# Trainium2, a two-layer decoder trunk in split fp32: the first weights and the first block of x in halves, another order of forms, warm-up products from a constant

## The chip, the cores and the metric

The kernel runs on one core of one Trainium2 chip, in one launch. The metric is the time of that launch on the device, in microseconds (us). An execution recorded by the profiler gives the trace and the profile from which rows are quoted. The engines in them are PE (TensorE, matrix products), PEld (its weight loads), DVE (VectorE), ACT (ScalarE), POOL (GpSimd) and SP (SyncE, which here only issues DMAs). A "q" behind an engine's name (SPq, POOLq) means the DMA queue that it feeds.

## What is computed

A residual stream x of 256 rows and 4096 columns goes through two layers, each with its RMS norm, and a final RMS norm:

```
def reference(x, norm_attn, w_in_attn, w_out_attn, norm_conv, w_in_conv, conv_w,
              w_out_conv, final_norm):
    h = x
    for i in range(DEPTH):
        if i % N_MIXERS == 0:
            h = h + attn_branch(rms_norm(h, norm_attn), w_in_attn, w_out_attn)
        else:
            h = h + conv_branch(rms_norm(h, norm_conv), w_in_conv, conv_w, w_out_conv)
    return rms_norm(h, final_norm)

def attn_branch(xn, w_in, w_out):
    proj = xn @ w_in
    q, k, v, g = jnp.split(proj, 4, axis=-1)
...
    o = stick_breaking_attention(to_heads(q), to_heads(k), to_heads(v))
...
    return (o * jax.nn.silu(g)) @ w_out
```

`DEPTH` is 1, so only the attention branch is computed: an input projection (256 x 4096 by 4096 x 16384), a causal attention of 32 heads of 128, a gate, an output projection (4096 x 4096), the residual sum, and the final norm with its gain. All inputs are float32.

## The kernel before

**Tiling.** The output of a projection is made in units (`units`, line 279): 16 units of `w_in`, each of two pairs of column blocks of 256, and then the units of `w_out`. A unit runs over 16 steps of the contraction (`NS`), each of 2 x 128 (`KT` = 2). For a step there are two tiles of weights, `raw{q}_{t}`, each 128 partitions x 2 column blocks x 2 contraction halves x 256 float32, 512 KB, fetched on SP's queue by two DMAs of one column block each (`load`, line 380). Seven such tiles can be in memory at once. All of x stays in memory as 16 blocks of 128 x 2 x 256 (`blocks_of`, line 553), one for each step.

**Split operands.** Every operand is used as a high part and a low part in a type of reduced precision: for weights, ACT casts `raw` into `wh` and DVE subtracts, giving `wl` (`piece`, line 451). x's forms in the first unit are `sh` and `sl`, in the other units `nh` and `nl`; those of the attention's output are `oh` and `ol`. A product is three matmuls of 512 columns into a bank `acc`: high by high, high by low, low by high (`mm3`, line 816). The numbers behind these names count the parts (`wl930` is the low part of part 930). Most steps are done with sums of blocks in seven products in place of eight (`SEVEN_PARTS`, line 84); for those DVE also forms sums of `raw` tiles (`sums`, line 424), and POOL adds one block onto another by a DMA that accumulates (`add_block`, line 401).

**What sets the order.** The products follow each other on PE in one list (`order`, line 306). Everything else is ordered by a planner (`Plan`, line 113), which simulates the engines with estimated costs while the program is written: a piece of work asks for buffers (`take`), waits until something is told (`until`, `tell`), and queues for its engine with a key, mostly the estimated time of the product that needs it. When an engine of the simulation comes free, the work with the lowest key is written into the real program (`turn`, line 229). On the chip each engine then executes its instructions in this order, and semaphores keep the true dependences. A different estimate or one more wait at the start thus can alter what the planner does anywhere behind it.

**The start.** x's block 0 takes the gain and one DMA of 256 KB on ACT's queue (lines 576 and 577). For each contraction half DVE forms `sh`, then waits for the low part of the weights of that half, then forms `sl` (lines 581 to 592). The first weight part (n = 0) is cut into halves (line 489) and its low part waits for `sh` (line 469), so that DVE makes `sh`, `wl`, `sl` twice. After that the raw block 0 is scaled with the gain by ACT (lines 597 to 601) for its sums. Blocks 1 to 3 of x are requested at fixed planned times (line 565). Ahead of the first product PE multiplies tiles of zeros, `idle`, into a bank `warm` that nobody reads; DVE sets each of the ten (lines 614 to 618).

**The end.** In the last unit the last five parts are kept, and their products run bank by bank in the order 5, 4, 2, 3 (`LAST_ORDER`, line 60). h stands in 16 tiles `h0` to `h7` for each of two halves of the rows, t = 0 and t = 1. `last_h` (line 1107) and `block_done` (line 1142) add the banks to h and the rows of x (`xres`); bank 3 is added to `h7` of t = 0 in two halves of 256 columns, behind the last products. For each t the sums of squares give a factor: `mean_before_last` (a reduce and a tensor_scalar), `joined` (a scalar_tensor_tensor), and in `finish` (line 1184) the `factor` of four operations, all on the tile `scalars`. `rows_out` (line 1206) then multiplies each tile of h by it, and SP stores the tile, 256 KB each. The rows of t = 1 are done first.

Almost all instructions bear one line number in the profile, L132, which is the helper that records them; the names of the tiles tell them apart.

Of the kernel before, what the change touches and what calls it, by code (L numbers as in the profile page):

```python
# [12 lines left out]
BF16 = mybir.dt.bfloat16  # L13
# [6 lines left out]
P = 128  # L20
S = 256
# [4 lines left out]
CW = 256  # L26
HG = CW // P
NB = D // CW
W = 2 * CW
NJ = D // W  # L30
KT = 2
# [6 lines left out]
BEHIND = {("turn", 0): ("eee", "eee")}  # L38
WARM, IDLE = 10, 640

# [12 lines left out]
ROWS = 4  # L53
# [195 lines left out]
def kernel(  # L249
# [10 lines left out]
    nc = Plan(tc)  # L260
# [50 lines left out]
    for g, (n, k) in enumerate(order):  # L311
        p = parts[n]
# [60 lines left out]
    raw, wh, wl = {}, {}, {}  # L373
# [6 lines left out]
    def load():  # L380
# [3 lines left out]
        for _, q, t in sorted(tiles):  # L384
            w, blocks, s = quads[q][t]
            if FORMS_BEHIND < q < NS:
                yield nc.until(("form", "s", q - FORMS_BEHIND))
            yield nc.take("raw")
            r = raw[q, t] = wp.tile([P, HG, KT, CW], F32, tag="raw", name=f"raw{q}_{t}", bufs=RAW_BUFS)
            if t and seven[q]:  # L390
                nc.start(add_block(q))

            def both():
                for i, c in enumerate(blocks):
                    nc.sync.dma_start(r[:, i], w[c, s])

            yield moved(
                "sync", both, [KT * CW] * HG, first[quad_parts[q][0]] + t, after=lambda q=q, t=t: nc.tell(("raw", q, t))
            )
# [51 lines left out]
    def piece(n, c, there):  # L451
# [16 lines left out]
        if n == 0:  # L468
            yield nc.until(("sh", c.start))
        yield dve(lambda: minus(l, full, h), size, key, more=10)  # L470
# [4 lines left out]
    def split(size, tag, bufs):  # L475
        for n, p in enumerate(parts):
# [4 lines left out]
            if size == KT:  # L481
                yield nc.take(tag)
            yield nc.until(("raw", q, t))
            if size < KT:
                yield nc.take(tag)
            wh[n] = halves(wp.tile([P, KT * W], F32R, tag="wh" if size == KT else "s", name=f"wh{n}", bufs=bufs))
            if size == 1:
                wh[n], wl[n] = wh[n][:, 0:1], wh[n][:, 1:2]
            cuts = [slice(k, k + 1) for k in range(KT)] if n == 0 else [slice(0, size)]
            lows_left[n] = len(cuts)  # L490
            if p["seven"] and p["i"] == 0:
                nc.start(sums(q))
            for c in cuts:
                nc.start(piece(n, c, [("sums", n)] if p["seven"] and p["i"] > 1 else [("raw", q, t)]))

# [57 lines left out]
    def blocks_of(i):  # L553
# [9 lines left out]
        if i:  # L563
            yield moved(
                "sync", lambda: nc.sync.dma_start(y, xT[i]), [KT * S], key - 1, hold=True, wait=1300 * i - 600 if i < 4 else 0
            )
# [8 lines left out]
        else:  # L575
            yield moved("scalar", lambda: nc.scalar.dma_start(gcol, gain_in), [KC], key - 1)
            yield moved("scalar", lambda: nc.scalar.dma_start(y, xT[i]), [KT * S], key - 1, hold=True)
            for c in range(KT):
                hc, lc = (t[:, 2 * c : 2 * c + 2, :].rearrange("p a b -> p (a b)") for t in (h, l))

                yield dve(
                    lambda: nc.vector.tensor_scalar(out=hc, in0=y[:, c, :], scalar1=gain(c), scalar2=None, op0=ALU.mult),
                    S, key - 1,
                )
                nc.tell(("sh", c))
                yield nc.until(("low", 0, c))
                yield dve(
# [3 lines left out]
                    S, key - 1,  # L591
                )
        nc.tell(("form", "s", i))
        later = place_at(0, i + BLOCKS_LATER)
        if not i:

            def scaled():
# [16 lines left out]
    warm = att.tile([P, W], F32, tag="att", name="warm")  # L614
    for k in range(WARM):
        idle = wp.tile([P, IDLE], BF16, tag="gh", name=f"idle{k}", bufs=ROWS)
        nc.vector.memset(idle, 0.0)
        nc.tensor.matmul(warm, idle[:, 0:P], idle[:, 0:W], start=True, stop=True)

# [195 lines left out]

    def mm3(out_, a, b, start, stop, orders):

        (ah, al), (bh, bl) = a, b
        for k, (x, y) in enumerate(((ah, bh), (ah, bl), (al, bh))):
            q, e = RUNS[orders[k]]  # L820
# [418 lines left out]
    def product(n, k):  # L1239
# [7 lines left out]
        elif p["i"] == 0 and k == 0:  # L1247
# [7 lines left out]
            ends[p["u"], b] == (n, k),  # L1255
            orders,
        )

# [80 lines left out]
```

## Time and profile before

| | before |
|---|---|
| median of three runs | 1693.62 us |
| the three runs | 1691.8, 1693.62, 1694.25 us |
| profiled execution: span from its first to its last instruction | 1691.3 us |
| median less that span | 2.3 us |
| DMA moved in the span | 412.78 MB, mean 244 GB/s |

The profiled execution is known by its span; the time around it is taken as the difference in the table's fourth row. In the rows that follow, a timeline's columns are the start in us, the length from the first instruction's start to the last one's end, engine, line, operation, output<-inputs with their shapes, and the number of instructions joined in the row (x10); in brackets stand the idle time ahead of it and what ended it. Rows of the waits give the total, the count and the longest. A row of windows gives the stretch and its length, then the busy time and the count of PE, PEld, DVE, ACT and POOL in this order, then the granted clock, the busy share of the DMA engines and their GB/s. Rows of transfers give the issuing queue, size, and us from issue to landing.

### The profile page before, as it was taken

Reading aid. Unit: us, or ns where it says so; the run is one execution under the profiler, and the core shown is the slowest. Engines: PE = TensorE matmul, PEld = TensorE weight load, DVE = VectorE, ACT = ScalarE, POOL = GpSimd, SP = SyncE. Lnnn points to the kernel's source line nnn. Section 1 sums busy time; section 2 is a strip of 40 time slices with the busy share of each in tenths; the row PEclk is TensorE's granted clock in tenths of the full one; section 3 lists DMA queues with packets and bytes.
Section 4 is the critical chain, followed back from the end, with each engine's and each line's share of the span. In section 5 each row is a group of like instructions: output and inputs, shape, how many; then the busy total and the mean of one; then the engine's idle time right before and its main releaser. Section 6 shows DMA issues by size and latency. Waiting matters only on the chain.

```text
span 1691.3 us, 25185 instructions
## 1 busy us (share of the span) xinstructions
PE 1675.4 (99%) x7776; PEld 1419.6 (84%) x7776; DVE 1599.4 (95%) x2025; ACT 1200.8 (71%) x1665; POOL 325.5 (19%) x400
## 2 busy tenths in 40 slices
PE   9999999999999999999999999999999999999996
PEld 7888888888888888888888888888888888888885
DVE  8889999999999999999999999999999987999997
ACT  8986767676767686867676767686867775666664
POOL 0012222222212222222222222212122111212110
PEclk9999999999999999999999999999999999999999
DMA  9978887889788979797979787878787877888895
GB/s 344 331 199 244 235 240 222 242 234 251 223 242 229 260 210 256 216 268 201 267 207 268 210 259 214 258 216 250 220 252 223 282 259 245 245 246 262 246 302 186
DMA packets 248440, 412.78 MB, mean 244 GB/s; under 512 B 28016, under 2 KB 72560, under 8 KB 248304
## 3 DMA queue, kind: packets, MB, share of 16 engines
q1 hardware_dynamic: 194544, 354.24, 62.6%
q0 software_dynamic: 53472, 56.65, 20.3%
q8 instruction: 61, 1.00, 0.2%
q14 instruction: 75, 0.61, 0.1%
q10 hardware_dynamic: 288, 0.28, 0.1%
HBM read 402.93 MB, written 8.13 MB: 243 GB/s over the span
## 4 chain that ended last, share of the span: by engine, by line
PE 97%; DVE 1%; DMA 1%; issue 0%; ACT 0%; SPq 0%; DVEq 0%; ACTq 0%
PE acc L132 92%; PE z L132 3%; PE o L132 1%; PE tr L132 1%; DMA raw<-in_w_in_dram 1%; DVE h L132 0%; DVE wl L132 0%; ACT wh L132 0%; DVE raw L132 0%; DVE scalars L132 0%; SPq L132 0%; DVE qk_sb L132 0%; ACT sq L132 0%; ACT scalars L132 0%; DVE sl L132 0%
## 5 line engine op out<-in xcount | busy, mean ns | idle before, releaser
L132 ACT CAST wh<-raw 128x1024 fp32r<-128x1024 f32 (+1 forms) x989 | 916.0, 969 | 375.9 <-DVE raw L132 166.2
L132 DVE TENSOR_TENSOR wl<-raw,wh 128x1024 fp32r<-128x1024 f32 (+1 forms) x815 | 967.4, 1216 | 44.6 <-ACT wh L132 25.3
L132 PE MATMUL acc<-wh,sh 128*128 128x512 f32 x2048 | 768.8, 387 | 0.3 <-DVE sh L132 0.3
L132 PE MATMUL acc<-wh,sl 128*128 128x512 f32 x1898 | 727.2, 383 | 0.1
L132 PE MATMUL acc<-wl,sh 128*128 128x512 f32 x1748 | 668.6, 382 | 0.0
L132 POOL DMA_DIRECT2D raw<-in_w_in_dram x300 | 259.0, 962 | 972.9 <-DMA raw<-in_w_in_dram 472.4
L132 PEld LDWEIGHTS acc<-wh,sh 128*128 128x128 f32 x2048 | 384.2, 188 | 69.1 <-ACT wh L132 1.2
L132 PEld LDWEIGHTS acc<-wh,sl 128*128 128x128 f32 x1898 | 356.0, 188 | 64.4 <-DVE sl L132 0.9
L132 PEld LDWEIGHTS acc<-wl,sh 128*128 128x128 f32 x1748 | 328.5, 188 | 56.8 <-DVE wl L132 0.4
L132 DVE TENSOR_TENSOR raw<-raw,raw 128x512 f32<-128x512 f32 x348 | 237.7, 683 | 7.6 <-DMA raw<-in_w_in_dram 5.9
L132 PE MATMUL acc<-wh,oh 128*128 128x512 f32 x512 | 192.2, 383 | 0.0
L132 PE MATMUL acc<-wh,ol 128*128 128x512 f32 x488 | 186.6, 382 | 0.0
L132 PE MATMUL acc<-wl,oh 128*128 128x512 f32 x464 | 177.4, 382 | 0.7 <-DVE wl L132 0.7
L132 DVE TENSOR_TENSOR wh<-raw,wh 128x512 fp32r<-128x512 f32 x174 | 118.7, 682 | 0.6 <-ACT wh L132 0.3
L132 DVE TENSOR_TENSOR raw<-raw 128x512 f32<-128x512 f32 x174 | 118.7, 682 | 0.0
L132 PEld LDWEIGHTS acc<-wh,oh 128*128 128x128 f32 x512 | 96.0, 187 | 17.2
L132 PEld LDWEIGHTS acc<-wh,ol 128*128 128x128 f32 x488 | 91.5, 187 | 16.1
L132 PEld LDWEIGHTS acc<-wl,oh 128*128 128x128 f32 x464 | 87.0, 188 | 16.9 <-DVE wl L132 1.4
L132 POOL DMA_DIRECT2D raw<-in_w_out_dram x48 | 41.7, 985 | 173.7 <-DMA raw<-in_w_out_dram 69.8
L132 ACT ACTIVATE f<-f 128x384 f32<-128x384 f32 x96 | 50.4, 525 | 3.0
L132 DVE SCALAR_TENSOR_TENSOR gv_sb<-acc,scalars,gv_sb 128x512 f32<-128x512 f32 x45 | 33.5, 744 | 0.3
L132 POOL DMA_DIRECT2D p<-spill x27 | 16.1, 662 | 87.8 <-ACT wh L132 27.1
(86 smaller groups left out, 765.3 us busy)
## 6 DMA issues: line engine op xcount, KB each, us to landing
raw<-in_w_in_dram SPq DMA_DIRECT2D x1024, 256.0 KB, 4.5
raw<-in_w_out_dram SPq DMA_DIRECT2D x256, 256.0 KB, 4.4
raw<-in_w_in_dram POOLq DMA_DIRECT2D x300, 128.0 KB, 5.3
p<-spill POOLq DMA_DIRECT2D x27, 256.0 KB, 4.8
raw<-in_w_out_dram POOLq DMA_DIRECT2D x48, 128.0 KB, 5.3
xr<-in_x_dram SPq DMA_DIRECT2D x16, 256.0 KB, 5.2
xres<-in_x_dram SPq DMA_DIRECT2D x16, 256.0 KB, 5.4
out_dram<-h SPq DMA_DIRECT2D x16, 256.0 KB, 2.9
```

The source lines that it names most:

```text
L132: return self.tc.keep_in_program_order(getattr(self.engine, name)(*args, **kw))
```

## The change

The diff makes five edits.

1. The first tile of weights, `raw0_0`, comes in four DMAs of 128 KB, contraction half by contraction half (both column blocks of half 0, then both of half 1), and each half is told by itself. x's block 0 comes in two DMAs of 128 KB on ACT's queue, one for each half.
2. DVE's order for the first part is `sh`, `sl`, `wl` for each half: `wl` waits until `sl` is told, and the next `sh` until that `wl` is done. The second part (n = 1) is cut into halves as well.
3. In the first part's products the order of the three matmuls is swapped to high by high, then `wh` by `sl`, then `wl` by `sh`: `a` in `mm3` is the x form, which is loaded as the stationary side of the call, and `b` the weights.
4. The warm-up products are eight of 512 columns and four of 128 columns, on a preset constant of ones in bf16; the ten tiles that DVE set are gone.
5. In the plan, blocks 1 to 3 of x are requested 900 ns later, and the scaling of block 0 waits until the low parts of part 1 are done.

```diff
-WARM, IDLE = 10, 640
+WARM, WARM_SHORT = 8, 4
...
+            if not q and not t:
+                for k in range(KT):
+
+                    def half(k=k, r=r, w=w, s=s, blocks=blocks):
+                        for i, c in enumerate(blocks):
+                            nc.sync.dma_start(r[:, i, k, :], w[c, s][:, k, :])
+
+                    yield moved("sync", half, [CW] * HG, k - KT, after=lambda k=k: nc.tell(("raw", 0, 0, k)))
+                continue
...
         if n == 0:
-            yield nc.until(("sh", c.start))
+            yield nc.until(("sl", c.start))
...
-            yield nc.until(("raw", q, t))
+            yield nc.until(("raw", q, t) if n else ("raw", 0, 0, 0))
...
-            cuts = [slice(k, k + 1) for k in range(KT)] if n == 0 else [slice(0, size)]
+            cuts = [slice(k, k + 1) for k in range(KT)] if n < 2 else [slice(0, size)]
...
-                nc.start(piece(n, c, [("sums", n)] if p["seven"] and p["i"] > 1 else [("raw", q, t)]))
+                nc.start(
+                    piece(n, c, [("sums", n)] if p["seven"] and p["i"] > 1 else [("raw", q, t) if n else ("raw", 0, 0, c.start)])
+                )
...
-                "sync", lambda: nc.sync.dma_start(y, xT[i]), [KT * S], key - 1, hold=True, wait=1300 * i - 600 if i < 4 else 0
+                "sync", lambda: nc.sync.dma_start(y, xT[i]), [KT * S], key - 1, hold=True, wait=1300 * i + 300 if i < 4 else 0
...
-            yield moved("scalar", lambda: nc.scalar.dma_start(y, xT[i]), [KT * S], key - 1, hold=True)
+            for c in range(KT):
+                yield moved(
+                    "scalar", lambda c=c: nc.scalar.dma_start(y[:, c, :], xT[i][:, c, :]), [S], key - 1,
+                    after=lambda c=c: nc.tell(("x", 0, c)),
+                )
...
+                yield nc.until(("x", 0, c), *([("low", 0, c - 1)] if c else ()))
...
-                nc.tell(("sh", c))
-                yield nc.until(("low", 0, c))
...
+                nc.tell(("sl", c))
...
         if not i:
+            yield nc.until(("lows", 1))
...
-    for k in range(WARM):
-        idle = wp.tile([P, IDLE], BF16, tag="gh", name=f"idle{k}", bufs=ROWS)
-        nc.vector.memset(idle, 0.0)
-        nc.tensor.matmul(warm, idle[:, 0:P], idle[:, 0:W], start=True, stop=True)
+    ones = tc.nc.const_aps.tensor(1.0, (P, W), BF16)
+    for k in range(WARM + WARM_SHORT):
+        n = W if k < WARM else P
+        nc.tensor.matmul(warm[:, 0:n], ones[:, 0:P], ones[:, 0:n], start=True, stop=True)
...
-    def mm3(out_, a, b, start, stop, orders):
+    def mm3(out_, a, b, start, stop, orders, swap):
...
-        for k, (x, y) in enumerate(((ah, bh), (ah, bl), (al, bh))):
+        pairs = ((ah, bh), (al, bh), (ah, bl)) if swap else ((ah, bh), (ah, bl), (al, bh))
+        for k, (x, y) in enumerate(pairs):
...
             orders,
+            not n,
```

The planner then writes the whole program in a somewhat different order. Three places on DVE follow, each of before and then of the change. In the rows a name is a tile with a running number behind it, output<-inputs, and the shape; `TENSOR_TENSOR` that reads `raw` and `wh` is the subtraction that makes `wl`.

DVE at the start of the program, before:

```order
L132 MEMSET idle9_126 128x320
L132 TENSOR_SCALAR sh0_79<-xs0_78,gcol_76 128x256
L132 TENSOR_TENSOR wl0_165<-raw0_0_81,wh0_159 128x512
L132 SCALAR_TENSOR_TENSOR sl0_80<-xs0_78,gcol_76,sh0_79 128x256
L132 TENSOR_SCALAR sh0_79<-xs0_78,gcol_76 128x256
L132 TENSOR_TENSOR wl0_165<-raw0_0_81,wh0_159 128x512
L132 TENSOR_TENSOR wl1_176<-raw0_1_95,wh1_170 128x1024
L132 SCALAR_TENSOR_TENSOR sl0_80<-xs0_78,gcol_76,sh0_79 128x256
```

The same place in the changed order:

```order
L132 TENSOR_SCALAR sh0_79<-xs0_78,gcol_76 128x256
L132 SCALAR_TENSOR_TENSOR sl0_80<-xs0_78,gcol_76,sh0_79 128x256
L132 TENSOR_TENSOR wl0_145<-raw0_0_81,wh0_140 128x512
L132 TENSOR_SCALAR sh0_79<-xs0_78,gcol_76 128x256
L132 SCALAR_TENSOR_TENSOR sl0_80<-xs0_78,gcol_76,sh0_79 128x256
L132 TENSOR_TENSOR wl0_145<-raw0_0_81,wh0_140 128x512
L132 TENSOR_TENSOR wl1_170<-raw0_1_126,wh1_160 128x512 x2
```

The memsets are gone, `sl` of a half stands ahead of its `wl`, and the second half's `sl` no longer stands behind the whole of `wl1`.

DVE in the output projection, about 120 us from the end, from the low part `wl927` on, before (`h3` is a tile of h that gets its rows of x; the rows that write `raw299` form sums of weight tiles):

```order
L132 TENSOR_TENSOR wl927_15217<-raw298_0_15072,wh927_15173 128x1024
L132 TENSOR_TENSOR raw299_0_15132<-raw299_0_15132,raw299_1_15085 128x2x256
L132 TENSOR_TENSOR wh935_15235<-raw301_1_15157,wh935_15235 128x512
L132 TENSOR_TENSOR raw299_1_15085<-raw299_0_15132,raw299_1_15085 128x2x256
L132 TENSOR_TENSOR h3_14702<-h3_14702,xres3_1_15199 128x512
L132 TENSOR_TENSOR raw299_0_15132<-raw299_0_15132 128x2x256
L132 TENSOR_TENSOR wl932_15255<-raw300_0_15145,wh932_15248 128x1024
L132 TENSOR_TENSOR wl930_15267<-raw299_1_15085,wh930_15216 128x1024
```

The same stretch in the changed order, from `wl927` to `wl930`, and behind it the rows, seven ahead of that `wl927`, where the add on `h3` now stands:

```order
L132 TENSOR_TENSOR wl927_15215<-raw298_0_15059,wh927_15162 128x1024
L132 TENSOR_TENSOR raw299_1_15077<-raw299_0_15119,raw299_1_15077 128x2x256
L132 TENSOR_TENSOR wh935_15224<-raw301_1_15153,wh935_15224 128x512
L132 TENSOR_TENSOR raw299_0_15119<-raw299_0_15119 128x2x256
L132 TENSOR_TENSOR wl932_15244<-raw300_0_15139,wh932_15231 128x1024
L132 TENSOR_TENSOR wl930_15252<-raw299_1_15077,wh930_15203 128x1024
```

```order
L132 TENSOR_TENSOR wl923_15151<-raw297_1_15005,wh923_15112 128x1024
L132 TENSOR_TENSOR raw298_0_15059<-raw298_0_15059,raw298_1_14988 128x2x256
L132 TENSOR_TENSOR h3_14689<-h3_14689,xres3_1_15127 128x512
L132 TENSOR_TENSOR raw298_1_14988<-raw298_0_15059,raw298_1_14988 128x2x256
L132 TENSOR_TENSOR wh929_15145<-raw299_1_15077,wh929_15145 128x512
```

Between `wl927` and `wl930` there were six rows and are four now: the add on `h3` and one sum on `raw299` moved ahead of `wl927`.

DVE at the end of the program, before, from the factor of t = 1 (the rows on `scalars`) on:

```order
L132 SCALAR_TENSOR_TENSOR scalars_77<-squares_of_rows_142,scalars_77 128x1
L132 SCALAR_TENSOR_TENSOR scalars_77<-scalars_77 128x1
L132 TENSOR_SCALAR scalars_77<-scalars_77 128x1
L132 TENSOR_TENSOR scalars_77<-scalars_77 128x1
L132 TENSOR_SCALAR h0_1_13993<-h0_1_13993,scalars_77 128x512
L132 TENSOR_SCALAR h2_14701<-h2_14701,scalars_77 128x512
L132 TENSOR_SCALAR h4_15418<-h4_15418,scalars_77 128x512
L132 TENSOR_SCALAR h5_1_15420<-h5_1_15420,scalars_77 128x512
L132 TENSOR_TENSOR h7_0_15594<-acc19_3_15530,h7_0_15594 128x256
```

The same place in the changed order:

```order
L132 TENSOR_TENSOR h7_0_15575<-acc19_3_15513,h7_0_15575 128x256 x2
L132 SCALAR_TENSOR_TENSOR scalars_77<-squares_of_rows_124,scalars_77 128x1
L132 SCALAR_TENSOR_TENSOR scalars_77<-scalars_77 128x1
L132 TENSOR_SCALAR scalars_77<-scalars_77 128x1
L132 TENSOR_TENSOR scalars_77<-scalars_77 128x1
L132 SCALAR_TENSOR_TENSOR scalars_77<-squares_of_rows_124,scalars_77 128x1
L132 TENSOR_SCALAR h0_1_13980<-h0_1_13980,scalars_77 128x512
L132 TENSOR_SCALAR h2_14688<-h2_14688,scalars_77 128x512
L132 TENSOR_SCALAR h4_15405<-h4_15405,scalars_77 128x512
L132 TENSOR_SCALAR h5_1_15407<-h5_1_15407,scalars_77 128x512
```

Both halves of the add of bank 3 to `h7` of t = 0, which before stood behind the first four scalings (one of them here, the other two rows later), now stand ahead of the factor of t = 1 and of all scalings.

## The prediction

> **What bounds the kernel now.** I read the page's first and fourth parts, then what TensorE (PE) waited for, then the timeline of both ends.
>
> ```profile
> span 1691.3 us, 25185 instructions
> ...
> PE 1675.4 (99%) x7776; PEld 1419.6 (84%) x7776; DVE 1599.4 (95%) x2025; ACT 1200.8 (71%) x1665; POOL 325.5 (19%) x400
> ...
> PE 97%; DVE 1%; DMA 1%; issue 0%; ACT 0%; SPq 0%; DVEq 0%; ACTq 0%
> ```
>
> PE is busy 99% of the span, and 97% of the chain that ended last is PE. A busy PE need not be a PE at its peak, so the waits come next:
>
> ```profile
> PE warm L132 <- DVE idle L132: 1.3, 1, 1.3
> PE acc L132 <- DVE wl L132: 0.7, 1, 0.7
> PE acc L132 <- DVE sh L132: 0.3, 1, 0.3
> ```
>
> Behind the head there is one wait of 0.7 us in 1.68 ms. So the time is three pieces: a head until the matmuls stream, the stream, and a tail behind the last matmul. The change doesn't alter how many products there are; it can move only the head, that one wait and the tail. Its order of instructions moves all three.
>
> **The head.** The rows of before, in order of time:
>
> ```profile
> 0.95 3.58 DVE L132 MEMSET idle<- 128x320 uint32 x10 [0.95 <-PEq L1326]
> 1.33 4.45 PE L132 MATMUL warm<-idle 128*128 128x512 bf16 x10 [1.33 <-DVE idle L132]
> 5.33 1.14 ACT L132 CAST wh<-raw 128x512 fp32r<-128x512 f32 x2 [3.25 <-DMA raw<-in_w_in_dram]
> 5.62 0.35 DVE L132 TENSOR_SCALAR sh<-xs,gcol 128x256 fp32r<-128x256 f32 x1 [1.09 <-DMA xs<-in_xT_dram]
> 6.12 0.76 PE L132 MATMUL acc<-wh,sh 128*128 128x512 f32 x1 [0.34 <-DVE sh L132]
> 6.73 0.80 PE L132 MATMUL acc<-wl,sh 128*128 128x512 f32 x1
> 7.33 0.63 PE L132 MATMUL acc<-wh,sl 128*128 128x512 f32 x1
> 7.47 1.05 ACT L132 CAST wh<-raw 128x1024 fp32r<-128x1024 f32 x1 [1.00 <-DMA raw<-in_w_in_dram]
> 7.75 0.63 PE L132 MATMUL acc<-wh,sh 128*128 128x512 f32 x1
> 9.89 1.04 ACT L132 CAST wh<-raw 128x1024 fp32r<-128x1024 f32 x1
> 10.23 0.73 PE L132 MATMUL acc<-wh,sl 128*128 128x512 f32 x1
> 10.79 0.41 PE L132 MATMUL acc<-wh,sh 128*128 128x512 f32 x1
> 11.04 0.40 PE L132 MATMUL acc<-wl,sh 128*128 128x512 f32 x1
> 11.74 0.39 PE L132 MATMUL acc<-wl,sh 128*128 128x512 f32 x1
> 12.00 1.22 DVE L132 TENSOR_TENSOR wl<-raw,wh 128x1024 fp32r<-128x1024 f32 x1
> 14.44 0.38 PE L132 MATMUL acc<-wl,sh 128*128 128x512 f32 x1
> ```
>
> The reader is to see two rates. From 7.33 to 7.75 one matmul of 512 columns takes 0.42 us; from 10.79 to 11.04 it takes 0.25, and 0.22 later. PE runs at half rate until about 10.75. The granted clock in the page is 1.0 all along, so this halving shows in the spacing alone. The matmul at 11.74 is the 14th product matmul, the one at 14.44 the 26th.
>
> What the change does here. The ten memsets (3.58 us of DVE, 0.36 each) go, and with them PE's first wait: the warm-ups may start near 0.9 instead of 1.33. Eight at 0.43 and four of a quarter of the columns at 0.11 take 3.9 us, so they end near 4.8. No work waited for DVE before 5.6, so the memsets themselves are worth nothing beyond that.
>
> The first half needs 256 KB of weights, 128 KB of x and the gain, where before 512 KB and 256 KB had to be in. What the first transfers took from issue to landing:
>
> ```profile
> xs<-in_xT_dram ACTq DMA_DIRECT2D x1, 256.0 KB, 4.2
> gcol<-in_gain_in_dram ACTq DMA_DIRECT2D x1, 16.0 KB, 3.2
> ```
>
> The gain, nearly empty, lands at 0.84 + 3.2 = 4.0, so no half is usable before 4.0. The other bound: x, 256 KB, took 1.0 more than the gain, so half of x saves 0.5 at least, and 5.6 becomes 5.1. I take 4.3, nearer the lower, because every operand's bytes are halved. Transfers of 1 KB a partition are not in these rows; if each costs what one of 2 KB does, nothing is gained (a rival below). One cast of 512 elements is 0.57 (1.14 for two), and PE followed its operands by 0.15, so the first product starts near 5.05 instead of 6.12 (bounds 4.8 and 5.85).
>
> The first three matmuls wait for sh, then sl, then wl. Before it was sh, wl, sl, with 0.61 and 0.60 between them. I keep these, since sl (0.48 us) is shorter than wl but wl then follows it. With 0.427 after that, the 13th starts at 5.05 + 1.21 + 10 x 0.427 = 10.5, and the 14th, with the rate doubling at 10.75 as before, near 10.9 instead of 11.74: **0.8 us gained** (0.4 from the late bound of 5.85; 1.1 from the early one).
>
> Also gone is the stall ahead of 10.23 (0.77 between two matmuls that take 0.43), where the second half's sl stood in DVE's queue behind a whole tile's wl. It cost little, since PE was still at half rate.
>
> What the gain may run into: the two scalings of x's first block (0.90 with their pair) now stand on ACT ahead of the cast at 9.89, and the second tile's cast in halves adds 0.1. If that tile lands 0.3 sooner, this cast starts at 9.9 + 0.9 + 0.1 - 0.3 = 10.6 and ends at 11.65, its wl (1.22) ends near 12.9, and the 26th matmul can start at 13.05, not 14.44. So **1.4 us caps** the head. The second tile itself, two issues further back in SP's queue (some 0.43 each), is read at 7.47 and needed by the 13th matmul at 10.5; the blocks of x that are issued later are needed later still. These cost nothing until they are 2 us late.
>
> The Trainium skill (TensorE: Matmul & The Clock Gate, section "What's actually happening") says that PE's clock is halved until one free-running window of about 3.4 us was busy, wherever the window's edges fall. The spacing above agrees that there are two rates, 0.43 and 0.22, and that 4.4 us of warm-ups from 1.33 did not raise it. By that rule a busy stretch from 0.9 to 4.8 holds more such windows, and the sum would then use the cap, 1.4, in place of 0.8; that outcome is the second rival.
>
> **The one wait in the stream.**
>
> ```profile
> 1571.12 0.69 DVE L132 TENSOR_TENSOR h<-h,xres 128x512 f32<-128x512 f32 x1
> 1572.32 4.63 DVE L132 TENSOR_TENSOR wl<-raw,wh 128x1024 fp32r<-128x1024 f32 x4
> 1573.68 0.40 PE L132 MATMUL acc<-wh,oh 128*128 128x512 f32 x1
> 1574.73 0.49 PE L132 MATMUL acc<-wl,oh 128*128 128x512 f32 x1 [0.66 <-DVE wl L132]
> ```
>
> Between 1573.68 and 1574.73 lies 1.05 us where 0.22 is usual: 0.83 lost, waiting for wl930, the second of the four. In the changed order the h add of 1571.12 (0.60 to the next row's start) stands 12 rows ahead of wl930, not in the stretch behind wl927. So wl930 comes about 0.6 sooner, more if DVE's idle time shrinks too: between nothing and 0.83 gained, I take **0.7**.
>
> **The tail.**
>
> ```profile
> 1676.24 0.22 DVE L132 SCALAR_TENSOR_TENSOR scalars<-scalars 128x1 f32<-128x1 f32 x1
> 1676.88 1.68 DVE L132 TENSOR_SCALAR h<-h,scalars 128x512 f32<-128x512 f32 x4
> 1677.39 10.29 SPq L132 DMA_DIRECT2D out_dram<-h  x16
> 1677.71 0.40 PE L132 MATMUL acc<-wh,ol 128*128 128x512 f32 x1
> 1678.47 0.42 DVE L132 TENSOR_TENSOR h<-acc,h 128x256 f32<-128x256 f32 x1
> 1679.46 0.41 DVE L132 TENSOR_TENSOR h<-acc,h 128x256 f32<-128x256 f32 x1
> 1679.79 0.15 DVE L132 SCALAR_TENSOR_TENSOR scalars<-squares_of_rows,scalars 128x1 f32<-128x1 f32 x1
> ```
>
> The last matmul ends at 1678.1. Before it ends, the rows of t=1 already have their factor (the scalars from 1676.24) and are scaled from 1676.88; the first of 16 stores is issued at 1677.39. Only then comes the add that needs the last bank, at 1678.47. In the changed order both halves of that add stand ahead of the four scalar operations that make the factor for t=1. DVE takes its queue in order, so it stands still until the last matmul is done.
>
> Step by step, with PE's end held: first half 1678.47, second half 0.33 later (1679.46 to 1679.79 is the distance behind such a half), scalars from 1679.13. Four of them took 0.9 in all before (0.64 from 1676.24 to 1676.88, and the first 0.25), then one more that now stands there, 0.17: scaling starts at 1680.2 instead of 1676.88, **3.3 us later**, and the first store with it. ACT's two scalings for t=1 wait for the same factor.
>
> What the stores have to spare:
>
> ```profile
> 1679.00:1681.00 2.00, 0.00 (x0) 0.00 (x0) 1.10 (x4) 1.39 (x6) 0.00 (x0) 1.00 1.03 385
> 1687.00:1689.00 2.00, 0.00 (x0) 0.00 (x0) 0.00 (x0) 0.00 (x0) 0.00 (x0) 0.50 1.02 382
> ```
>
> From 1679 to 1689 the 16 DMA engines are full (share above 1, some 380 GB/s). 16 x 262 KB at 0.381 MB/us is 11.0 us: the stores bound the tail, not the work that feeds them, and what starts 3.3 later ends 3.3 later. Less is possible where the first stores, which then find several tiles ready, close ranks: bounds 2.7 and 3.5, I take **3.1**.
>
> **The sum.** 0.8 and 0.7 gained, 3.1 lost: 1.6 us longer. The span of 1691.3 becomes 1692.9. The median of the runs is 1693.62, which leaves 2.3 around the span; with the same around it the forecast is **1695.2**. By the bounds: from -1.4 - 0.83 + 2.7 = +0.5 to -0.4 + 0 + 3.5 = +3.1, so 1694.1 to 1696.7.
>
> **The rivals.**
> - *The tail hides its move*: the factor of t=1 would be no earlier anyway, or the stores catch up. Against it: the factor stood ready 1.8 us ahead of 1678.47, and the engines of the stores are full. Then 0.8 + 0.7 are won: 1692.1. Chance 0.12.
> - *PE's rate doubles before the first products.* For it: warm-ups start 0.4 sooner without a wait, and the gap behind them shrinks. Against: 4.4 us of them did not do it before. The head wins its cap, 1.4: 1.0 longer, 1694.6. Chance 0.25. This is the rule of the skill cited above.
> - *The halves land no sooner* (1 KB rows move at half the rate): the head wins nothing, so 3.1 - 0.7: 1696.0. Chance 0.10.
> - *Slower: the output stage gives the head start back.*
>
> ```profile
> 1500.00:1575.00 75.00, 74.34 (x336) 62.59 (x335) 71.63 (x85) 46.82 (x58) 14.22 (x17) 1.00 0.83 247
> ```
>
> DVE is busy 71.6 of 75 us here, and wl930 was late. If its 3.4 us of idle time are waits for data rather than for PE, DVE can't follow a PE that comes 0.8 sooner; PE then waits that long, and a low part formed one place later than before (one wl, 1.14 to the next) is paid in full. It decides as soon as PE reaches a part with no slack left, as at wl930. 3.1 + 1.1 with nothing won: 1697.8. Chance 0.08.
>
> **How the numbers follow.** The forecast has 0.42, the rivals 0.12, 0.25, 0.10 and 0.08, and 0.03 is left for what I don't see. A measurement can tell about 0.2% (3.4 us) from no change: below 1690.2 faster, above 1697.0 slower. All but the last rival lie within. Same 0.88; slower 0.09 (the last rival and the upper edge of the third); faster 0.03 (the lower edge of the first). For 8 in 10 the range reaches from just below the first rival to just above the forecast's late bound: 1692.0 to 1697.2.
>
> **What would show it.** In the timeline of after: the first product near 5.05, its spacing 0.43 until about 10.7 (or 0.22 at once: second rival); the 14th matmul 0.8 earlier; no wait of PE on wl near 1572; the first store 2.5 to 2.8 us behind the last matmul's end instead of 0.7 ahead of it, and the span's end 16 instead of 13.2 us behind it. A first store still ahead of PE's end would refute the tail, and with it the sign. New waits of PE between 1500 and 1670 would be the last rival.

## The result and the profile after

| | before | after |
|---|---|---|
| median of 15 runs each | 1693.96 us (1691.47 to 1696.53) | 1696.58 us (1695.66 to 1697.93) |
| ratio | | 1.0017, 95% interval 1.0010 to 1.0024 |
| span of the profiled execution | 1691.3 us | 1694.8 us |
| last matmul's end (its start and its length) | 1678.1 | 1679.1 |
| from there to the span's end | 13.2 | 15.6 |

The change makes the kernel 2.6 us longer by the medians. The prediction was 1695.2 us, in a range of 1692.0 to 1697.2, and no difference that a measurement can tell at 0.2%: that held. Its sum did not: of the three terms the tail was right in its cause, the head ran into another limit than the sum took, and a fourth term was missing. By the spans the sum was further off than by the medians (1692.9 forecast, 1694.8 measured). The profiled execution of the change took 1696.47 us, 1.7 more than its span; with the same 1.7 that of before would have taken 1693.0, about 1.0 less than its median.

Three slow runs (1756.63 us in x_sooner, 3766.14 in both_later, 2472.6 of the kernel before) count in the medians of the experiments below, but not in the ratios. The ratios are not the quotients of these medians.

The page of the changed kernel (its span, the busy times, the chain that ended last):

```profile
span 1694.8 us, 25182 instructions
...
PE 1676.3 (99%) x7778; PEld 1418.8 (84%) x7778; DVE 1604.5 (95%) x2016; ACT 1204.2 (71%) x1666; POOL 325.0 (19%) x400
...
PE 94%; DVE 2%; DMA 2%; issue 1%; ACT 1%; SPq 0%; DVEq 0%; ACTq 0%
```

PE's share of the chain falls from 97% to 94%. That is no measure of the loss: of the 100 us from 1500 to 1600 the chain now has PE for 29.0% (94.6% before), since it runs back over DVE and the transfers of `w_out` from a short wait of PE at 1575, and that wait costs less than the one before did (below). What PE waited for (total us, times, longest):

```profile
PE acc L132 <- DVE wl L132: 1.2, 2, 0.9
PE warm L132 <- PEq L1344: 0.8, 1, 0.8
PE acc L132 <- ACT wh L132: 0.6, 2, 0.3
```

To see where time goes, I number the matmuls into `acc` in the order of the trace (7158 in each kernel) and compare the start of the same one in two profiles. Negative is earlier than in the first profile of before:

| start of matmul number | 1 | 27 | 41 | 385 | 740 | 4645 | 6420 | 6775 | 7158 | then to the end |
|---|---|---|---|---|---|---|---|---|---|---|
| before | 6.12 | 14.66 | 17.74 | 94.0 | 177.8 | 1100.7 | 1513.6 | 1593.3 | 1677.7 | 13.2 |
| after | -1.41 | -0.58 | -0.50 | -0.44 | +0.01 | +1.70 | +1.63 | +0.65 | +1.02 | 15.6 |

So PE starts 1.4 sooner, keeps 0.5 of it, loses 2.1 in the stream between 385 and 4645, almost all of it without a wait, wins 1.0 around the wait of 1574, loses 0.4 of that again, and the tail adds 2.4.

**The head.** The timeline of the changed kernel:

```profile
0.85 4.00 PE L132 MATMUL warm<-const-bfloat16-1.0 128*128 128x512 bf16 x12 [0.85 <-PEq L1344]
4.70 0.74 PE L132 MATMUL acc<-wh,sh 128*128 128x512 f32 x1
5.26 0.41 PE L132 MATMUL acc<-wh,sl 128*128 128x512 f32 x1
6.06 0.39 PE L132 MATMUL acc<-wh,sh 128*128 128x512 f32 x1
6.29 0.38 PE L132 MATMUL acc<-wh,sl 128*128 128x512 f32 x1
8.60 0.50 PE L132 MATMUL acc<-wh,sh 128*128 128x512 f32 x1 [0.29 <-ACT wh L132]
10.44 0.91 ACT L132 ACTIVATE xs<-xs,gcol 128x256 f32<-128x256 f32 x2
11.25 1.03 ACT L132 CAST wh<-raw 128x1024 fp32r<-128x1024 f32 x1
11.29 1.27 DVE L132 TENSOR_TENSOR xs<-xs 128x128 f32<-128x128 f32 x4
12.33 0.49 PE L132 MATMUL acc<-wh,sh 128*128 128x512 f32 x1 [0.30 <-ACT wh L132]
12.47 1.22 DVE L132 TENSOR_TENSOR wl<-raw,wh 128x1024 fp32r<-128x1024 f32 x1
13.75 0.49 PE L132 MATMUL acc<-wl,sh 128*128 128x512 f32 x1 [0.93 <-DVE wl L132]
```

From 6.06 to 6.29 a matmul takes 0.23: the rate had doubled by then, not at 10.7. PE then outruns its operands twice, at the second tile (8.60) and at the third (12.33 and 13.75).

**The tail.** DVE and SP behind the last matmul:

```profile
1678.73 0.40 PE L132 MATMUL acc<-wh,ol 128*128 128x512 f32 x1
1679.16 0.76 DVE L132 TENSOR_TENSOR h<-acc,h 128x256 f32<-128x256 f32 x2 [1.58 <-PE acc L132]
1679.83 0.15 DVE L132 SCALAR_TENSOR_TENSOR scalars<-squares_of_rows,scalars 128x1 f32<-128x1 f32 x1
1680.73 1.67 DVE L132 TENSOR_SCALAR h<-h,scalars 128x512 f32<-128x512 f32 x4
1681.24 9.97 SPq L132 DMA_DIRECT2D out_dram<-h  x16
```

DVE stands still for 1.58 us until the last bank is done, then makes the factor of t = 1; the first store is issued 2.1 us behind the last matmul's end (1679.13) where it was 0.7 ahead of it.

**The wait at 1574.** The same two matmuls in the changed kernel:

```profile
1574.97 0.40 PE L132 MATMUL acc<-wh,oh 128*128 128x512 f32 x1
1575.45 0.49 PE L132 MATMUL acc<-wl,oh 128*128 128x512 f32 x1
```

They are 0.48 us apart, where 0.22 is usual and 1.05 was before.

**The stream.** Two windows of 400 us in which PE is busy almost throughout, of before and then of after (busy time and count, PE first):

```profile
400.00:800.00 400.00, 400.00 (x1880) 340.26 (x1880) 387.26 (x466) 291.69 (x394) 84.82 (x101) 1.00 0.83 236
800.00:1200.00 400.00, 399.81 (x1872) 339.61 (x1871) 386.32 (x462) 287.31 (x384) 84.32 (x100) 1.00 0.83 235
```

```profile
400.00:800.00 400.00, 400.00 (x1876) 339.64 (x1876) 388.63 (x464) 291.73 (x392) 84.19 (x99) 1.00 0.83 236
800.00:1200.00 400.00, 400.00 (x1869) 339.69 (x1868) 389.99 (x465) 290.12 (x385) 84.63 (x100) 1.00 0.83 236
```

The same 400 us hold four matmuls fewer in the first window (400 / 1880 = 0.21 us each, 0.85 in all) and three in the second, with a granted clock of 1.00 and a DMA share of 0.83 in both. This loss shows in no wait, and no line of the page points at it. From number 1095 to 4645 it is 838.92 us before and 840.51 after: 0.16 for each unit of 355 matmuls, ten times over. One total of this stretch is not enough to tell such a loss: two other profiles with the order of before took 839.81 (before_again) and 840.95 us (warm_alone), but there it lies in single stalls, of 1.87 us near 1015 in the second, and the rest of their units are as short as in before.

### The profile page after: what moved, and what is told of

Its sections match the earlier page's. It is cut to its first block, busy times and chain, and to the rows that moved or that the text cites. A ratio compares the mean times of both kernels' runs of the same rounds, so it can differ in the third digit from the quotient of the medians.

```text
span 1694.8 us, 25182 instructions
## 1 busy us (share of the span) xinstructions
PE 1676.3 (99%) x7778; PEld 1418.8 (84%) x7778; DVE 1604.5 (95%) x2016; ACT 1204.2 (71%) x1666; POOL 325.0 (19%) x400
## 4 chain that ended last, share of the span: by engine, by line
PE 94%; DVE 2%; DMA 2%; issue 1%; ACT 1%; SPq 0%; DVEq 0%; ACTq 0%
PE acc L132 89%; PE z L132 3%; PE o L132 1%; DMA raw<-in_w_out_dram 1%; DVE wl L132 1%; PE tr L132 1%; DVE h L132 1%; ACT wh L132 0%; DVE raw L132 0%; DMA raw<-in_w_in_dram 0%; DVE wh L132 0%; SPq L132 0%; DVE scalars L132 0%; DVE xs L132 0%; ACT xs L132 0%
## 5 line engine op out<-in xcount | busy, mean ns | idle before, releaser
L132 ACT ACTIVATE a<-z 128x384 f32<-128x384 f32 x32 | 15.7, 491 | 24.5 <-PE z L132 23.8
```

The lines of the kernel that those rows point to most:

```text
L132: return self.tc.keep_in_program_order(getattr(self.engine, name)(*args, **kw))
```

## Experiments

The rows of PE's order show one thing that differs in each unit: the attention's scores of the second head (`z`) stand 6 matmuls behind its transposes (`tr`) in all but the first and the last units; before it was 9. `product` (line 1239) gives the seven products behind such a piece fixed orders of columns (`BEHIND_OTHERS`), with an entry of its own for two products behind the first head's transposes, `BEHIND`. The theory: at a distance of 6 these orders fit badly. The rivals were other engines' traffic and the clock.

**words_turn1**: only the column orders behind the second head's transposes, on the changed kernel.

```diff
-BEHIND = {("turn", 0): ("eee", "eee")}
+BEHIND = {("turn", 0): ("eee", "eee"), ("turn", 1): ("eee", "eee")}
```

> Only the column order in which two products write their bank is altered, behind the second head's four transposes of each unit; every engine's order stays that of the change. Theory: the stream loses 0.16 us per unit because the scores of the second head now stand 6 matmuls behind its transposes (9 before) while the column orders behind them fit a distance of 9. Then 355 products take 83.83 to 83.88 us again as before (83.99 in the change), the stream wins 1.2 to 1.6 us and the time is 1695.1. Rival: the matmuls are slower because of other engines' traffic, or of the clock; then nothing changes, 1696.6.

Measured: 1694.11 us, ratio to before 1.0006 (0.9997 to 1.0014). From number 1095 to 4645 it took 838.98 us, 0.06 more than before. Its window holds the 1880 matmuls of before again:

```profile
400.00:800.00 400.00, 400.00 (x1880) 340.36 (x1880) 388.85 (x465) 291.98 (x394) 85.03 (x100) 1.00 0.82 236
```

One unit shows the place. In the changed kernel's timeline, from the transposes to the scores, and from there to the next piece (31 matmuls later):

```profile
784.76 0.60 PE L132 MATMUL tr<-ident,qk_sb 128*128 128x128 f32 x4
...
786.56 0.81 PE L132 MATMUL z<-qkT 128*128 128x128 f32 x4
...
794.80 0.34 PE L132 MATMUL z<-fh,neg_tri 128*128 128x384 f32 x1
```

And with the other orders of columns:

```profile
783.51 0.60 PE L132 MATMUL tr<-ident,qk_sb 128*128 128x128 f32 x4
...
785.37 0.82 PE L132 MATMUL z<-qkT 128*128 128x128 f32 x4
...
793.40 0.34 PE L132 MATMUL z<-fh,neg_tri 128*128 128x384 f32 x1
```

The first piece takes 1.80 and 1.86 us, the second 8.24 and 8.03: the same matmuls in the same place take 0.21 less, and 0.06 is paid ahead of it. The theory holds, and traffic and clock are out, since neither was touched. Over all runs it is as clear: the stretch from 1095 to 4645 took 840.52 us in the three profiles with a distance of 6 and the old column orders (after, tail_kept, warm_undone), and 838.99 to 839.05 in the six with the new ones.

**tail_kept**: the add of the last bank waits in the plan for the factor of t = 1 and is put behind four scalings.

```diff
-        yield nc.until(("full", LAST, b), *(["C12"] if b == 3 else ()))
+        yield nc.until(("full", LAST, b), *(["C12", ("factor", 1)] if b == 3 else ()))
...
-            yield add(h[:, cut], bank[b][:, cut], h[:, cut], late - 2, cut.stop - cut.start)
+            yield add(h[:, cut], bank[b][:, cut], h[:, cut], late + (105.5 if b == 3 else -2), cut.stop - cut.start)
```

> The add of the last bank to h7 of t = 0 waits in the plan for the factor of t = 1 and stands behind four scalings, as before the change; head and stream keep the order of the change. Theory: the tail's 2.5 us come from this place in DVE's queue alone. Then the first store is issued before the last matmul ends, the span ends 13.2 us behind that end instead of 15.7, and the time is 1694.1. Rival: the stores take as long from PE's end anyway, since the DMA engines are full; then 1696.6.

Measured: 1694.82 us, ratio 1.0009 (1.0000 to 1.0018). The timeline of its end:

```profile
1678.57 1.68 DVE L132 TENSOR_SCALAR h<-h,scalars 128x512 f32<-128x512 f32 x4
1678.68 0.40 PE L132 MATMUL acc<-wh,ol 128*128 128x512 f32 x1
1679.09 10.00 SPq L132 DMA_DIRECT2D out_dram<-h  x16
1680.16 0.42 DVE L132 TENSOR_TENSOR h<-acc,h 128x256 f32<-128x256 f32 x1
```

The span of 1692.6 ends 13.5 us behind the last matmul's end (1679.08), not 15.6. So 2.1 of the tail's 2.4 us hang on this place in DVE's queue; all six profiles with this edit have a tail of 13.55 to 13.57 us, the three others with the change's order there 15.6. The first store comes with PE's end, not 0.7 ahead of it, which goes with the 0.3 that stays.

**warm_alone**: the new warm-up products on the kernel before (the fourth edit alone).

> The kernel before with the new warm-up products alone; all orders are those of before. Theory: warm-ups that start near 0.85 without a wait raise PE's rate before the first product, so that matmuls from 6.7 on follow each other in 0.22 us; the wait for the second half's low part of x (10.23) stays, so only about 0.3 us are won behind it: the 26th product matmul 0.3 sooner, stream and tail the same, 1693.7 against 1694.0. Rival: the rate rises with the products, not the warm-ups; then spacings stay 0.43 until 10.7 and nothing is won.

Measured: 1692.7 us, ratio 0.9997 (0.9988 to 1.0006): no difference that can be told. In the profile the matmuls follow each other in 0.22 from 7.04 on, and matmul 27 came 0.68 sooner (0.3 was expected), the wait for the second `sl` remaining. The theory seemed to hold, until its counterpart:

**warm_undone**: the change with the old warm-up products.

> The change with the old warm-up products on zeros that DVE sets; all orders are those of the change but for the ten memsets. Theory: the operands of parts 1 and 2 bound the head, so a PE at half rate until 10.7 loses little: the 13th product matmul comes near 10.2 in place of 8.6, the 26th by at most 0.3 later than in the change (14.08), and the time stays within 0.3 of the change, 1696.6 to 1696.9. Rival: the new warm-ups are what won the head's 0.5; then the 26th comes 0.5 or more later and the time is 1697.1 or more.

Measured: 1696.33 us, ratio 1.0018 (1.0009 to 1.0027), as the change. Matmul 27 came 0.40 later than in the change, where at most 0.3 was expected, and matmul 41 only 0.10 earlier than in the first profile of before. But the rate had doubled here too, while the old warm-ups ran: the ten took 3.88 us. So the run with a late rate that was expected didn't come about, the new warm-ups aren't needed for an early one, and I asked the kernel before once more.

**before_again**: the kernel before, a second profile.

> The kernel before, profiled a second time. Theory: the moment at which PE's rate doubles belongs to the execution, not to the program (10.75 in the first profile of it, 4.6 in that of the change with the same old warm-ups); it may come anywhere from 4.5 to 11, and the time of 40 products differs from the first profile by no more than 0.7, since operands bound it. The stream's 355 products take 83.83 us again and the tail 13.2 us. Rival: the rate rises at 10.7 again, so the program sets it.

```profile
1.33 3.97 PE L132 MATMUL warm<-idle 128*128 128x512 bf16 x10 [1.33 <-DVE idle L132]
...
7.71 0.38 PE L132 MATMUL acc<-wh,sh 128*128 128x512 f32 x1
7.93 0.38 PE L132 MATMUL acc<-wl,sh 128*128 128x512 f32 x1
8.14 0.38 PE L132 MATMUL acc<-wh,sl 128*128 128x512 f32 x1
```

The ten warm-ups take 3.97 us here and took 4.45 in the first profile: the rate rose while they ran, in the same program. The moment belongs to the execution. The traces' own records of the granted clock say the same: the first of them, at 1.00, begins at 10.74 us in the first profile of before and at 4.67 in this one. The views count the time ahead of the first record as full speed, which is why the page showed 1.0 all along. This agrees with what the Trainium skill (TensorE: Matmul & The Clock Gate, section "What's actually happening") says of a free-running window and of a moment that varies from run to run. By the same section of the Trainium skill the moment varies by 500 ns either way; here one program has it at 4.67 and at 10.74. Matmul 41 was 0.58 earlier than in the first profile, so the first profile had a late rate, and the change's 0.50 need not be the change's at all. The tail took 13.2 us again.

**warm_ones**: the kernel before with warm-up tiles set to one in place of zero.

> The kernel before with warm-up tiles set to one, not to zero; nothing else differs. Theory: PE's rate depends on when it was busy, not on the numbers it multiplies: the first product comes at 6.1 and the rate rises as late as in the kernel before (10.7), or at a moment that differs from run to run, but not with the warm-ups as such. Rival: products of zeros don't count as work; then the rate rises by 6.3, as with the new warm-ups.

This run doesn't answer its question. A memset to one took 0.67 us, to zero 0.36, so the warm-ups came every 0.67 us with gaps and ended 2.6 us later, and the rate rose only near 12.9. Its time in one run was 1695.13 us.

**x_sooner**: the request times of x's blocks 1 to 3 as before (part of the fifth edit undone).

```diff
-wait=1300 * i + 300 if i < 4 else 0
+wait=1300 * i - 600 if i < 4 else 0
```

> The change with the requests of x's blocks 1 to 3 at their old planned times. The order then has 9 matmuls between transposes and scores of the second head again, the tail of before, and the add on h3 again between wl927 and wl930. Theory: the stream's 2.1 us and the tail's 2.5 us are gone, the wait at wl930 (0.7 to 0.8) is back, and the head loses 0 to 1.0 because wl1 stands behind two forms of x's block 1; 1692.7 to 1694.0, so no slower than before. Rival: the halves and the order of forms cost the stream or the tail by themselves; then it stays above 1695.5.

Measured: 1694.78 us, ratio 1.0008 (0.9999 to 1.0017), above the expected 1692.7 to 1694.0 and below the rival's 1695.5. Distance 9 and the tail of before are back in the order, and in the profile the tail takes 13.0 us and the units 83.8 again, but for one stall of 1.2 us near 346; the wait at 1574 is back as well, with 1.08 us between two matmuls. So, with the other edits in place, 900 ns in the plan of three requests at the start decided both of the change's losses, from some 120 us on and at the very end. The head is worse (matmul 41 comes 0.27 later than before): the low part of the second tile stands behind two forms of x's block 1 and PE waits at once for it.

```profile
8.72 1.27 DVE L132 TENSOR_TENSOR xs<-xs 128x128 f32<-128x128 f32 x4
9.91 1.29 DVE L132 TENSOR_TENSOR wl<-raw,wh 128x512 fp32r<-128x512 f32 x2
10.65 0.50 PE L132 MATMUL acc<-wl,sh 128*128 128x512 f32 x1 [1.58 <-DVE wl L132]
```

**tail_words** and **tail_words_2**: both edits on the change, in two sets of runs.

> Both earlier edits together on the change: the column orders behind the second head's transposes, and the add of the last bank behind four scalings. Theory: the two losses are separate places and add up, 2.0 from the stream and 2.2 from the tail; the head keeps its 0.5 to 0.9 before the kernel before; 1692.4, that is 1.0 to 1.5 below the kernel before of the same chip. Rival: one hides behind the other; then 1694 or more.

> The kernel with the two edits (column orders, place of the last add) once more, for the interval: theory 1692.4, 1.0 to 1.2 below the kernel before; rival: its gain was chance and it equals the kernel before within 0.3.

Measured: 1692.42 us against 1693.57 (ratio 0.9999, 0.9991 to 1.0008), and 1691.90 against 1692.95 (0.9994, 0.9985 to 1.0003). The two losses are separate and add up: both profiles have 13.6 us of tail and 839.05 us from number 1095 to 4645. Both medians are 1.1 us below the kernel before, but both intervals take in 1, and by the means of its runs the first set is only 0.1 below; that it is faster is not shown.

**all3**, **sums_later** and **both_later** try to free the head's operands on top of those two edits: in all3 the scaling of block 0 waits for the low part of part 2, in sums_later the four sums of x's block 1 do, in both_later both.

```diff
-            yield nc.until(("lows", 1))
+            yield nc.until(("lows", 2))
...
+        if i == 1:
+            yield nc.until(("lows", 2))
         yield from sums_of(i, y4, "n", later)
```

> Those two, and the scaling of x's block 0 waits until the low part of part 2, not of part 1, is done. Theory: in the change the cast of the third weight tile stood behind two scalings of 0.90 us on ACT and began 1.36 us after its tile had landed; with one of them moved behind it, the cast begins 0.8 sooner, the wait of PE on wl near 13 shrinks by 0.6 to 1.0, and the time is 1691.7. Rival: the next tile's landing (one each 1.34 us) or the forms of x's blocks then hold PE at the next part; then no better than with the two edits alone.

> All three edits before, and the four sums of x's block 1 wait until the low part of part 2 is done. Theory: in the run with the scaling moved, the cast of the third tile began 0.8 sooner but its low part still stood behind these sums (1.27 us) in DVE's queue and began at 12.50 as in the change (12.47); with the sums behind it, it begins at 11.5, the second product of that tile (26th) comes near 12.8 and not 14, and PE's lead on the kernel before is 1.3 to 2.0 by product 40. The time is 1691.5 to 1692.5. Rival: what the head wins is given back at later parts or in the output projection; then 1693 or more.

> As the one before, but the scaling of x's block 0 stays where the change has it, ahead of the cast. Theory: the cast then begins at 11.25 and the low part at 12.3, so moving the sums alone wins 0.2 at most on the run with two edits; lead by product 40 0.7 to 1.2, time 1692.2. Rival: the sums alone held the low part; then the 26th product comes as early as with both.

The first moved the cast forward as expected, and won nothing. Its rows:

```profile
10.45 1.05 ACT L132 CAST wh<-raw 128x1024 fp32r<-128x1024 f32 x1
11.30 1.27 DVE L132 TENSOR_TENSOR xs<-xs 128x128 f32<-128x128 f32 x4
12.50 1.22 DVE L132 TENSOR_TENSOR wl<-raw,wh 128x1024 fp32r<-128x1024 f32 x1
13.77 0.49 PE L132 MATMUL acc<-wl,sh 128*128 128x512 f32 x1 [1.43 <-DVE wl L132]
```

The low part starts at 12.50 as in the change (12.47), behind the sums in DVE's queue; my expectation had looked at ACT alone. With both moved:

```profile
9.93 1.05 ACT L132 CAST wh<-raw 128x1024 fp32r<-128x1024 f32 x1 [0.25 <-DMA raw<-in_w_in_dram]
11.01 1.23 DVE L132 TENSOR_TENSOR wl<-raw,wh 128x1024 fp32r<-128x1024 f32 x1 [0.61 <-ACT wh L132]
12.29 0.49 PE L132 MATMUL acc<-wl,sh 128*128 128x512 f32 x1 [0.45 <-DVE wl L132]
```

Here the cast follows the landing at last, and matmul 27 is 2.03 earlier than before. The lead was then lost again, before any tail, as the rival of both_later said (the table goes against the first profile of before, with its late rate):

| start of matmul number | 1 | 27 | 41 | 385 | 740 | 4645 | 6420 | 7158 |
|---|---|---|---|---|---|---|---|---|
| before_again | +0.16 | -0.58 | -0.58 | -0.58 | -0.58 | +0.30 | -0.30 | -0.67 |
| words_turn1 | -1.51 | -0.92 | -0.85 | -0.78 | -0.03 | -0.13 | -0.68 | -0.21 |
| tail_kept | -0.93 | -1.49 | -1.38 | -1.20 | -0.95 | +0.68 | +0.61 | +0.97 |
| tail_words | -0.74 | -1.31 | -1.16 | -0.93 | -0.49 | -0.45 | -1.01 | -0.13 |
| tail_words_2 | -0.84 | -1.11 | -0.98 | -0.82 | -0.66 | -0.62 | -1.18 | -0.96 |
| all3 | -1.51 | -0.56 | -0.42 | +0.61 | +1.39 | +1.42 | +0.87 | +2.56 |
| both_later | -0.85 | -2.03 | -1.41 | -0.47 | +0.42 | +0.44 | -0.12 | -0.66 |
| sums_later | -0.84 | -1.13 | -1.11 | -0.50 | -0.05 | -0.02 | -0.58 | -1.41 |

The times were 1694.02 (all3, ratio 1.0004, 0.9995 to 1.0013), 1692.98 (sums_later, 1.0004, 0.9995 to 1.0013) and 1693.25 us (both_later, 1.0005, 0.9996 to 1.0014): none is better than tail_words, and all miss their expected times. What takes the lead between numbers 41 and 740 I didn't try. In sums_later the rate rose only near 10.1, with the new warm-ups; behind its first product PE then shows no wait for an operand in the head, and its lead at number 41 (-1.11) is that of the two runs of tail_words (-1.16 and -0.98). In those, with an early rate, PE waited 0.9 us for `wl` at the third tile. So the two limits of the head, operands and rate, lie close together.

## Why the prediction was right, and where its sum was wrong

- **That it ends a little slower, within 0.2%**: right, by 2.6 us against the 1.6 forecast (3.5 by the spans).
- **The tail, +3.1 (2.7 to 3.5)**: the mechanism held and tail_kept shows it; the size was 2.4, below its own range. The step that failed is "with PE's end held: first half 1678.47". That add stood at 1678.47 because DVE was busy with four scalings from 1676.88, not because of PE. Freed of them it starts 0.03 behind the last matmul (1679.16), not 0.36, and the scaling 1.6 behind it, not 2.1. The stores then close ranks by some 0.4. (The factor of before was ready at 1676.84, 1.6 ahead of 1678.47 and not 1.8, which changes nothing.)
- **The head, -0.8**: measured -0.50 at number 41 in the profile of after. The five profiles of kernels that share its head (after, words_turn1, tail_kept, tail_words, tail_words_2) give -0.97 in the mean, from -0.50 to -1.38, all with an early rate. The two of before give 0 and -0.58. That is 0.4 won against before_again, which had an early rate too, and up to 1.0 against the first profile; the changed head with the old warm-ups (warm_undone) has -0.10. So a gain is likely, but it is not clear of what differs from one execution to the next.
- **The working behind that head** failed. The first product came at 4.70, just outside the bounds of 4.8 to 5.85: the gain landed at 3.2 (0.84 and 2.4 us), not at 4.0 as the lower bound took it, and the first cast began at 3.95. The 14th matmul came 2.4 earlier (9.33) where 0.8 was forecast, and most of that was lost again by the 27th. The step "with the rate doubling at 10.75 as before" failed: the rate rises at a moment that changes with the execution, and it came at 5.28 here. The page of the profile hides this, since the granted clock there is 1.0 all along; the trace's records begin only with the doubling. The other half of that part, the cap (scalings ahead of the third tile's cast, 26th matmul no sooner than 13.05), was then the limit. It came at 13.75, since the scalings began at 10.44 and the cast at 11.25 in place of 10.6, and sums of x in DVE's queue held the low part some 0.2 more. The rival with an early rate had the early rate right and gave the head the whole cap, 1.4. Its reason is not shown: the new warm-ups took 4.0 us, less than the 4.45 that did not raise the rate, and the old ones raised it early in two other profiles.
- **The wait at 1574, -0.7 (0 to 0.83)**: the mechanism as drawn, with 0.26 us lost there (0.48 less 0.22) instead of 0.83, so 0.57 won. Part of the gain around it went at other low parts in the output projection: number 6775 is 0.98 earlier relative to 6420, number 7158 then 0.37 later. In tail_words PE comes 1.0 early to 6420 and leaves with 0.13. That stage takes back part of a lead, as the last rival said; which of DVE's rows is late in each case I didn't try.
- **The stream**: the sentence that "it can move only the head, that one wait and the tail" is the step of the sum that failed. Order on PE was among the things the change moved, and the distance between attention's pieces and the column orders fitted to it cost 0.16 in each unit, 1.7 us from number 740 on, shown by words_turn1, and by x_sooner the other way round. A further 0.45 between 385 and 740 holds 0.3 of a wait of the output product behind `gated` on ACT; that part was only read from the trace.

By terms: -0.50 (head, to number 41) + 2.13 (to 6420) - 0.98 + 0.37 + 2.4 = 3.4, against 3.5 between the spans. That the forecast came near is in part luck: a head that gained less and a stream that lost 2.1 were partly set off by a smaller tail and a larger gain around 1574, and the time around the span of before (2.3) held some 0.6 of that one execution.

## What to carry to other kernels

When a program's order is planned from estimates, a shift of under a microsecond at the start is a change to every place behind it: compare the whole order on the engine that bounds, not only the queues that feed it, and pin by a rule what must not move (a wait in the plan for the factor, an order of columns for each distance). Where the busy time is 99%, count instructions in equal windows: a slower stream shows there and in no wait. A head that gets its first operands sooner is worth only what the second and third operands allow, on each queue they pass.

## What the runs showed of the hardware

- The spacing of PE's matmuls fell from 0.43 to 0.22 us at another moment in each execution, and at that moment the trace's records of the granted clock begin: 10.74 and 4.67 us in two profiles of the kernel before, 5.28 in that of the change, 10.09 in sums_later, whose warm-ups are those of the change. A page of the profile counts the time ahead of the first record as 1.0. In the kernel before, matmul 41 came 0.58 us sooner in the profile with the early rate.
- The stretch at full clock lasted 1669.12, 1672.53, 1675.94 or 1679.36 us in the 14 traces, in steps of 3.41 us; it ended at a granted clock of 0.50, from 2.1 to 5.3 us behind the last matmul.
- Matmuls of equal size and unchanged operands took 8.24 or 8.03 us for one run of them, by the order in which two earlier products write the columns of their bank (0.16 us a unit, in all profiles with the one order or the other).
- A memset of a 128 x 640 bf16 tile took 0.36 us for zero, recorded as 320 words of 32 bits, and 0.67 for one, recorded as 640 elements of 16 bits.
